# Where the gate's early load stands in the queue, fourth buffers for the output stage, and one more pair done with seven products

## The chip, the cores and the metric

The kernel runs on one core of one Trainium2 chip. Its engines work side by side and in order, each through its own list: TensorE (matrix products; PE in the profile, its weight loads PEld), VectorE (DVE), ScalarE (ACT), GpSimd (POOL) and SyncE (SP), which issues most of the DMA transfers. An engine that waits holds up what is behind it in its own list, and only that. The metric is the device time of one execution in microseconds; lower is better. All times below are microseconds unless marked ns. In the rows of the profile "L786" is line 786 of the kernel before.

## The reference

One decoder layer on 256 tokens of width 2048, everything in float32:

```python
h = rmsnorm(x, norm_g)                                   # (256, 2048)
shift, scale, gate = split(silu(c) @ ada_w + ada_b, 3)   # 3 x 2048
h = h * (1 + scale) + shift
b, cg, v, g = split(h @ w_in, 4)                         # w_in: 2048 x 4*4096
u = causal_depthwise_conv(cg * v, conv_w)                # width 3, per channel
y = b * u * silu(g)                                      # (256, 4096)
out = rmsnorm(x + gate * (y @ w_out), final_g)           # w_out: 4096 x 2048
```

The two large products dominate: h @ w_in with 128 MB of weights, and y @ w_out with 32 MB. `ada_w` is another 48 MB.

## The kernel before

**Precision.** Each large operand is split into a high part, which ScalarE casts to float32r (`split_hi`, L380), and a low part, the difference, which VectorE makes (`split_lo`, L385). A product is then three matmuls: high x high, high x low, low x high.

**The first product, first half.** The 4096 channels go in 32 columns of 128. The first 16 columns run in chunks while `ada_w` streams in (`part`, L573; bank `mm_s`); the orders of SyncE, VectorE and ScalarE there are written out by hand as strings of letters (L656 to L667). The tokens lie transposed in SBUF as `hT`, 16 blocks `k` of 128 model columns, each with a high and a low part (`tokens`, L322): blocks 0 to 13 in one tile with the tag "big", 14 and 15 in one with the tag "big2".

**The first product, second half** (L798 to L836, bank `mm_b`). Eight pairs of columns, for each the four quarters of `w_in` in the order c, v, g, b, for each quarter two loads of 1 MB with eight token blocks: 64 *pieces* of 48 matmuls with 256 columns. A piece is a load into `raw` (L804), its split into `hi` and `lo`, and the products; each piece goes twice through its eight blocks, once for each column of the pair. `raw`, `hi` and `lo` each go round three buffers (`w_tile`, L145). Behind each piece stand a call of `gate_piece` and one of `early_weights`.

`gate_piece` (L692) adds up the gate part of `ada_w`; at the end of each of four groups of 512 columns GpSimd folds the 128 partitions in seven steps, each with two DMAs and an addition (L713 to L717), and a last DMA adds the result to `gate_row` in DRAM (L719).

`early_weights` (L775) prepares parts of the output stage and stores them in DRAM (`made`). What is done behind which piece stands in `EARLY` (L761): behind pieces 35, 39, ... 55 the sums for pairs 10 to 15, behind piece 58 the load of the gate's last 512 columns on all partitions (`turned`, L786), behind 59 and 62 the weights of two units times that gate. The place of `turned` is also used by the fold. Outside the parts ordered by hand, a scheduler of the language, with its own picture of the times, chooses the order in each engine's list; `tc.add_manual_dep(..., after, ...)` orders two instructions of one engine without a semaphore.

**The second product** (the output stage, L838 on). `w_out` is used in pairs of 128-row blocks. `columns` (L943) runs 1024 output columns: the first 1024 with all 16 pairs, the second 1024 with 12 pairs, and the remaining weights of the second in four units of four blocks (`LAST`, each half of the columns for itself). A full pair is 24 matmuls with 512 columns. A pair in `SEVEN` or `SEVEN_2` is done as a Strassen-like scheme with seven block products, 21 matmuls (`seven`, L904): it needs sums of the tokens (`token_forms`, L729), sums of the weights (`sums_of`, L767) and splits of both the weights and the sums. In the first 1024 columns the sums of the weights are made on the spot; in the second they come from `made`. `gather` (L933) adds up the banks of the sevens.

Buffers of the output stage before: raw weights and sums share `wide_ring` (L857) in the first 1024 columns, three `lo` buffers and three places in `big`, the old token tile, up to n = 12, then the three `lo`; in the second `next_ring` (L1017), three `lo` and one place in `big`. Casts go round the three `hi`, low parts round the three `raw` buffers. `load_ends` (L863) puts loads for the end among the weights of the first 1024 columns: the gate's first half at n = 11 (`AT_END - 2`), half of `x` at n = 13, the final weights and the gate's second half at n = 14. The second half of `x` follows at n = 8 of the second columns (`AT_X`).

**The end.** With the gate already multiplied into the weights of the last 512 columns, the residual and the partial results go into PSUM first (`move`, L1042), and the last products are added there (`out_mm(po[t], ...)`), while VectorE and ScalarE do the rest of the final norm (`third`, `finish`).

Of the kernel before, what the change touches and what calls it, by code (L numbers as in the profile page):

```python
# [13 lines left out]
P = 128  # L14
D = 2048
# [102 lines left out]
def short_conv_layer(ctx: ExitStack, tc: tile.TileContext, x, c, norm_g, ada_w, ada_b, w_in, conv_w, w_out, final_g, out):  # L118
# [20 lines left out]

    nth = {"raw": 0, "hi": 0, "lo": 0}  # L140

    def pad(n, name, pool=wpool):
# [155 lines left out]
    rstd = const.tile([P, TT], F32, tag="rstd", name="rstd")  # L298
    junk = hpool.tile([P, TT, HX], F32, tag="big", name="junk")
    for t in range(TT):  # L300
# [16 lines left out]

    KB = KT - 2
    hT = hpool.tile([P, KB, 2 * T], F32R, tag="big", name="hT")
    hT2 = hpool.tile([P, KT - KB, 2 * T], F32R, tag="big2", name="hT2")  # L320

    def tokens(k, part):  # L322
        return (hT[:, k] if k < KB else hT2[:, k - KB])[:, part * T : (part + 1) * T]

# [351 lines left out]
    def gate_columns(c0, n):  # L676
        flat = gate_slots[c0 // 1024].rearrange("p h s f -> p (h s f)").bitcast(F32)
# [5 lines left out]
    def load_gate(j):  # L683

        c0 = j * 1024
        nc.sync.dma_start(gate_columns(c0, 1024), gate_row[0:1, c0 : c0 + 1024].partition_broadcast(P))

# [36 lines left out]
    SEVEN = range(8, 16)  # L724
    SEVEN_2 = range(10, 16)
    forms = {}
# [38 lines left out]
    passed = [0]  # L765

    def sums_of(b, s):  # L767
# [7 lines left out]
    def early_weights():  # L775

        while to_store:
            unit, sums = to_store.pop()
            made[unit] = dram.tile([P, SLOT], F32, tag=f"made{len(made)}", name="made")
            nc.scalar.dma_start(made[unit], sums)  # L780
        unit = EARLY.get(passed[0])
        passed[0] += 1
        if unit is None:
            return
        if unit == "gate":
            nc.sync.dma_start(turned, gate_row[0:1, 3 * W : 4 * W].partition_broadcast(P))  # L786
            return
        raw, sums = raw_tile("raw_u"), w_tile("lo", "sums_u")
        blocks, out = (v.rearrange("p (b f) -> p b f", f=W) for v in (raw, sums))
        if not isinstance(unit, int):  # L790
            load_o(raw, unit[1] * EP, EP, 3 * W, W)
            nc.vector.tensor_tensor(out=out, in0=blocks, in1=turned.unsqueeze(1).to_broadcast([P, EP, W]), op=ALU.mult)
        else:
            load_o(raw, 2 * unit, 2, 2 * W, 2 * W)
            list(sums_of(blocks, out))
        to_store.append((unit, sums))

    for ct in range(NS, NCT, 2):  # L798
        for q in QUARTERS:
            bank = psum.tile([P, CT, T], F32, tag="mm", name="mm_b")[:, 0:2]  # L800
            col = q * E + ct * P
            for kp in range(0, KT, KP):
                raw = raw_tile("raw")
                nc.sync.dma_start(  # L804
                    raw.rearrange("p (k f) -> p k f", k=KP),
# [32 lines left out]

    big = hpool.tile([P, 3 * D + W], F32, tag="big", name="big")
    xh = big[:, 0 : TT * D].rearrange("p (h t f) -> p h t f", h=2, t=TT)  # L840
    HD = D // 2

    def xr(t, c0, n):
        return xh[:, c0 // HD, t, c0 % HD : c0 % HD + n]

    def load_x(h):
        for t in range(TT):
            nc.sync.dma_start(xh[:, h, t], x[t * P : (t + 1) * P, h * HD : (h + 1) * HD])

    fg = big[:, TT * D : 3 * D]  # L850
    u2 = big[:, 3 * D :]
    ends = [z.rearrange("p a b f -> p (a b f)").rearrange("p (h f) -> p h f", h=2) for z in zs]

    places6 = [None] * 3 + [big[:, i * SLOT : (i + 1) * SLOT] for i in range(3)]
    taken, ending = [0], [False]

    def wide_ring(name):  # L857

        i = taken[0] % 6 if not ending[0] else 0
        taken[0] += 1  # L860
        return w_tile("lo", name) if places6[i] is None else places6[i]
# [12 lines left out]
    last_silu = ended_silu[0]  # L874
    warm2 = const.tile([P, 1], F32, tag="fs", name="warm2", bufs=2)
# [21 lines left out]
    def weighted(t, c0, n, pr, at):  # L897


        r = xr(t, c0, n)  # L900
        nc.scalar.activation(pr, r, AF.Square, scale=D**-0.5, accum_out=fsq[:, t, at : at + 1])
        nc.vector.tensor_tensor(out=r, in0=r, in1=fg[:, c0 : c0 + n], op=ALU.mult)

# [38 lines left out]

    def columns(c0, order, sevens, bank, p1, p6, p75, whole, loads=None, ring=None):  # L943


        for n, j in enumerate(order):
            raw = w_tile("raw", "raw_o") if n == 0 and c0 == 0 else ring("raw_o")
            ready = c0 > 0 and j in made
# [9 lines left out]
            if j in sevens:  # L958
                sums = ring("sums_o")
                if ready:  # L960
                    nc.sync.dma_start(sums, made[j])
                seven(j, raw, sums, ready, bank, p1, p6, p75, j == sevens[0], j == sevens[-1])
                if j == sevens[-1]:
                    gather(p1, p6, p75)
                continue
# [14 lines left out]
    def wide_bank(name):  # L980
# [5 lines left out]
        0, (0, 1, 8, 2, 9, 3, 10, 4, 11, 5, 12, 13, 6, 14, 15, 7), SEVEN,  # L986
        lambda t, d: wide[t][:, d], *extra_banks(), p75, True, load_ends, wide_ring,
    )
# [9 lines left out]
    def finish(t):  # L998
# [4 lines left out]
        for c0, n, vector in ((0, 512, True), (512, 512, False), (1536, 512, True), (1024, 512, False)):  # L1003
            dd = slice(c0, c0 + n)
            r = xr(t, c0, n)
            if c0 == 1536:
                nc.vector.scalar_tensor_tensor(out=r, in0=po[t], scalar=fs, in1=fg[:, dd], op0=ALU.mult, op1=ALU.mult)
# [7 lines left out]
    taken[0] = 0  # L1015

    def next_ring(name):  # L1017

        i = taken[0] % 4
        taken[0] += 1  # L1020
        return big[:, SLOT : 2 * SLOT] if i == 3 and taken[0] <= 12 else w_tile("lo", name)
# [88 lines left out]
```

## Time and profile before

| | us |
|---|---|
| runs without the profiler (3), median | 920.08 (919.80 to 920.12) |
| the profiled execution | 917.02 |
| its span, first to last instruction | 915.2 |
| TensorE busy | 888.6 (97%) |
| VectorE busy | 695.4 (76%) |
| ScalarE busy | 490.5 (54%) |
| GpSimd busy | 88.0 (10%) |

The profile of the chip lists every instruction with its start, its length and what ended the idle time before it. Busy shares are means over stages with different limits, so the stages are read one by one. By the first and last matmuls of each stage, the first half of the first product runs from 24.4 to 376.8, the second half from 376.9 to 740.2, and the output stage's matmuls from 740.23 to 907.9. In a row such as `L385 DVE TENSOR_TENSOR lo<-raw,hi 128x2048 ... x66 | 153.3, 2328 | 78.6 <-ACT hi L380 63.1` the numbers behind the first bar are the busy time of the group and the mean length of one in ns, and behind the second the idle time of the engine just before them and what ended most of it. A row `PE mm_b L545 <- ACT hi L380: 11.4, 1, 11.4` of the waits says who waited for whom, the sum, how often, and the longest.

### The profile page before, as it was taken

How to read it: one execution, taken by the hardware profiler on the slowest of the kernel's cores; microseconds unless marked ns; L12 is line 12 of the kernel's file. 1: busy time of each engine (PE TensorE's matmuls, PEld its weight loads, DVE VectorE, ACT ScalarE, POOL GpSimd, SP SyncE). 2: the span in 40 equal slices, each digit the busy share in tenths (PEclk: the TensorE clock that was granted, in tenths of full speed). 3: DMA queues.
4: the chain of work that ended last, by engine and by line, in shares of the span. 5: the costliest groups of instructions: out<-in, count | busy, mean ns of one | idle time of the engine just before them, and what ended most of it. 6: DMA issues, size and time to landing. Idle time of an engine off the chain costs nothing.

```text
span 915.2 us, 16520 instructions
## 1 busy us (share of the span) xinstructions
PE 888.6 (97%) x6977; PEld 849.9 (93%) x6977; DVE 695.4 (76%) x693; ACT 490.5 (54%) x436; POOL 88.0 (10%) x108
## 2 busy tenths in 40 slices
PE   7999999999999999999999999949999999999996
PEld 4999999999999999999999999949999988778885
DVE  5889998889987876858865786537667668999775
ACT  6768866565558765644344434234434454545553
POOL 0000000010000234410132012400000000000000
PEclk9999999999999999999999999979999999999999
DMA  9999999999997688777877889489889877686872
GB/s 307 368 370 365 365 321 354 341 363 351 380 344 258 189 279 238 237 215 222 271 230 219 273 270 307 142 286 301 290 286 289 306 264 244 197 294 235 302 280 92
DMA packets 164873, 257.29 MB, mean 281 GB/s; under 512 B 7668, under 2 KB 106580, under 8 KB 162624
## 3 DMA queue, kind: packets, MB, share of 16 engines
q1 hardware_dynamic: 159680, 239.89, 79.5%
q0 software_dynamic: 3840, 7.94, 3.2%
q10 hardware_dynamic: 1280, 8.43, 2.3%
q8 instruction: 54, 0.88, 0.4%
q14 instruction: 19, 0.16, 0.0%
HBM read 237.86 MB, written 10.50 MB: 271 GB/s over the span
## 4 chain that ended last, share of the span: by engine, by line
PE 79%; DMA 11%; DVE 4%; ACT 2%; POOL 2%; issue 1%; SPq 0%; ACTq 0%; POOLq 0%; DVEq 0%
PE mm_s L545 38%; PE mm_b L545 27%; PE mm_o L888 6%; PE mm L888 4%; DMA z<-gacc 3%; PE mm_w L888 3%; DMA at_g<-in_ada_w_dram 3%; DVE lo L385 2%; DMA at<-in_ada_w_dram 2%; ACT hi L380 2%; POOL gacc L717 1%; DMA raw_o<-in_sc_w_out_dram 1%; DMA raw<-in_sc_w_in_dram 1%; POOL z L715 0%; DVE gacc L711 0%
## 5 line engine op out<-in xcount | busy, mean ns | idle before, releaser
L545 PE MATMUL mm_b<-hT,hi 128*128 128x256 f32 x2048 | 349.9, 277 | 11.4 <-ACT hi L380 11.4
L545 PE MATMUL mm_s<-hT,hi 128*128 128x256 f32 x2048 | 336.3, 277 | 0.0
L545 PEld LDWEIGHTS mm_b<-hT,hi 128*128 128x128 f32 x2048 | 309.3, 188 | 11.6 <-ACT hi L380 11.6
L545 PEld LDWEIGHTS mm_s<-hT,hi 128*128 128x128 f32 x2048 | 299.7, 188 | 0.2
L545 PE MATMUL mm_b<-hT,lo 128*128 128x256 f32 x1024 | 283.4, 277 | 1.5 <-DVE lo L385 1.5
L545 PE MATMUL mm_s<-hT,lo 128*128 128x256 f32 x1024 | 261.7, 277 | 0.0
L380 ACT CAST hi<-raw 128x2048 fp32r<-128x2048 f32 (+1 forms) x66 | 123.8, 1876 | 206.9 <-PE mm_b L545 94.0
L385 DVE TENSOR_TENSOR lo<-raw,hi 128x2048 fp32r<-128x2048 f32 (+1 forms) x66 | 153.3, 2328 | 78.6 <-ACT hi L380 63.1
L545 PEld LDWEIGHTS mm_b<-hT,lo 128*128 128x128 f32 x1024 | 192.9, 188 | 1.8 <-DVE lo L385 1.8
L545 PEld LDWEIGHTS mm_s<-hT,lo 128*128 128x128 f32 x1024 | 182.7, 188 | 0.0
L385 DVE TENSOR_TENSOR lo<-raw_s,hi 128x2048 fp32r<-128x2048 f32 (+1 forms) x80 | 149.0, 1868 | 29.9 <-ACT hi L380 29.3
L380 ACT CAST hi<-raw_s 128x2048 fp32r<-128x2048 f32 (+2 forms) x81 | 124.0, 1541 | 70.2 <-PE mm_s L545 42.9
L515 DVE SCALAR_TENSOR_TENSOR gv<-at,silu_c,gv 128x512 f32<-128x512 f32 x105 | 78.8, 751 | 10.3 <-DMA at<-in_ada_w_dram 8.6
L568 ACT COPY acc<-mm_s 128x1024 f32<-128x1024 f32 x54 | 54.6, 1011 | 26.9 <-PE mm_s L545 26.8
L717 POOL TENSOR_TENSOR gacc<-gacc,z 128x512 f32<-128x512 f32 x28 | 44.2, 1577 | 103.4 <-DMA z<-gacc 103.4
L888 PE MATMUL mm_w<-hi,y 128*128 128x512 f32 x160 | 51.4, 390 | 0.3 <-ACT hi L380 0.3
L711 DVE SCALAR_TENSOR_TENSOR gacc<-at_g,silu_c,gacc 128x512 f32<-128x512 f32 x60 | 45.0, 749 | 7.4 <-DMA at_g<-in_ada_w_dram 6.3
L888 PE MATMUL mm_o<-hi,y 128*128 128x512 f32 x152 | 48.3, 389 | 0.0
L582 ACT COPY mm_s<-acc 128x1024 f32<-128x1024 f32 x38 | 38.6, 1015 | 2.6 <-DVE acc L571 1.8
L380 ACT CAST hi<-raw_o 128x2048 fp32r<-128x2048 f32 x14 | 26.7, 1909 | 22.1 <-DMA raw_o<-in_sc_w_out_dram 16.8
L385 DVE TENSOR_TENSOR lo<-raw_o,hi 128x2048 fp32r<-128x2048 f32 x14 | 32.1, 2289 | 6.8 <-ACT hi L380 6.7
L888 PEld LDWEIGHTS mm_w<-hi,y 128*128 128x128 f32 x160 | 30.0, 188 | 6.9 <-ACT hi L380 0.7
(191 smaller groups left out, 745.6 us busy)
## 6 DMA issues: line engine op xcount, KB each, us to landing
raw<-in_sc_w_in_dram SPq DMA_DIRECT2D x64, 1024.0 KB, 6.2
raw_s<-in_sc_w_in_dram SPq DMA_DIRECT2D x47, 1024.0 KB, 8.2
at<-in_ada_w_dram SPq DMA_DIRECT2D x126, 256.0 KB, 7.9
raw_o<-in_sc_w_out_dram SPq DMA_DIRECT2D x17, 1024.0 KB, 6.0
raw_s<-in_sc_w_in_dram SPq DMA_DIRECT2D x33, 512.0 KB, 7.2
at_g<-in_ada_w_dram SPq DMA_DIRECT2D x32, 512.0 KB, 8.2
raw_u<-in_sc_w_out_dram SPq DMA_DIRECT2D x8, 1024.0 KB, 5.7
made<-sums_u ACTq DMA_DIRECT2D x8, 1024.0 KB, 6.9
```

Of the source, the lines that this page charges most:

```text
L380: nc.scalar.copy(hi[:, :n], raw[:, :n])
L385: last_low[0] = nc.vector.tensor_tensor(out=lo[:, :n], in0=raw[:, :n], in1=hi[:, :n].bitcast(F32), op=ALU.subtract)
L515: nc.vector.scalar_tensor_tensor(out=gv, in0=at4[:, i], scalar=c_k, in1=gv, op0=ALU.mult, op1=ALU.add)
L545: mm = last_mm[0] = nc.tensor.matmul(dst, w, h[k], start=begins and left, stop=ends, skip_group_check=True)
L568: nc.scalar.copy(acc[ch, q], bank)
L582: nc.scalar.copy(bank, acc[ch, q])
L711: nc.vector.scalar_tensor_tensor(out=ga, in0=at3[:, i, :], scalar=s, in1=ga, op0=ALU.mult, op1=ALU.add)
L717: nc.gpsimd.tensor_tensor(out=ga, in0=ga, in1=turned, op=ALU.add)
L888: nc.tensor.matmul(dst, y[a], b, start=opens and i == 0, stop=ends and i == 2, skip_group_check=True)
```

## The change

- The gate's early load is put at piece 55 and tied: it can be issued only behind the load of that piece's weights. The units of `early_weights` come three pieces earlier (32, 36, ... 52; 56 and 60).
- The token tile `big` becomes four tiles b0 to b3. In the output stage b0, b1 and b2 serve as fourth buffers of `lo` (raw weights and sums), `hi` (casts) and `raw` (low parts). In the first 1024 columns all three kinds have four up to n = 10, then three; from n = 13 on `lo` has four again, with b1, up to n = 5 of the second columns. The rings of six and of four are gone.
- `x` goes into b0 and b1, the final weights and the gate's first half share b2 (`closing`), and the gate's second half goes into the first gate slot. The loads at n = 13 are half of `x`, half of the final weights and the gate's first half; at n = 8 of the second columns the other half of `x`, the gate's second half, and the other half of the final weights, which takes the place of the gate's first half.
- Pair 9 joins the sevens of the second columns; its sums are made on the spot. The order there becomes 0, 10, 1, 11, 2, 9, 3, 12, 13, 8, 14, 15; first and last of the sevens are taken from that order.

```diff
     def w_tile(kind, name, dtype=F32, i=None):
         if i is None:
-            i = nth[kind] % 3
-            nth[kind] += 1
+            size = 4 if kind in fourth else 3
+            i = nth[kind] % size
+            nth[kind] = i + 1
+        if i == 3:
+            return hpool.tile([P, SLOT + 64], dtype, tag=fourth[kind], name=name)[:, 16 : 16 + SLOT]
...
-    KB = KT - 2
-    hT = hpool.tile([P, KB, 2 * T], F32R, tag="big", name="hT")
-    hT2 = hpool.tile([P, KT - KB, 2 * T], F32R, tag="big2", name="hT2")
+    hT = [hpool.tile([P, SLOT + 64], F32R, tag=f"b{g}", name="hT") for g in range(3)]
+    hT += [hpool.tile([P, 4 * T], F32R, tag=tag, name="hT") for tag in ("b3", "big2")]
...
-    SEVEN_2 = range(10, 16)
+    SEVEN_2 = range(9, 16)
...
-    EARLY = {35 + 4 * i: j for i, j in enumerate(SEVEN_2)}
-    EARLY.update({58: "gate", 59: ("gated", LAST[0]), 62: ("gated", LAST[1])})
+    EARLY = {32 + 4 * i: j for i, j in enumerate(range(10, 16))}
+    EARLY.update({55: "gate", 56: ("gated", LAST[0]), 60: ("gated", LAST[1])})
...
         if unit == "gate":
-            nc.sync.dma_start(turned, gate_row[0:1, 3 * W : 4 * W].partition_broadcast(P))
+            load = nc.sync.dma_start(turned, gate_row[0:1, 3 * W : 4 * W].partition_broadcast(P))
+            tc.add_manual_dep(load.ins, last_load[0].ins.name, after, reason="the gate is done by then")
...
     def load_x(h):
+        xh.append(hpool.tile([P, TT, HD], F32, tag=f"b{h}", name="xr"))
...
+    def load_broadcast(c, src):
+        nc.sync.dma_start(closing[0][:, c : c + HD], src.partition_broadcast(P))
+
+    def load_fg(h):
+        load_broadcast(h * HD, final_g.rearrange("(o d) -> o d", o=1)[:, h * HD : (h + 1) * HD])
...
     def load_ends(n):
-        ending[0] = n >= AT_END
-        if n == AT_END - 2:
-            load_gate(0)
+        if n == AT_END - 3:
+            fourth.clear()
         elif n == AT_END:
             load_x(0)
-        elif n == AT_END + 1:
-            nc.sync.dma_start(fg, final_g.rearrange("(o d) -> o d", o=1).partition_broadcast(P))
-            load_gate(1)
+            closing.append(hpool.tile([P, D], F32, tag="b2", name="closing"))
+            load_fg(0)
+            load_broadcast(HD, gate_row[0:1, 0:HD])
+            fourth["lo"] = "b1"
+
+    fourth.update({"lo": "b0", "hi": "b1", "raw": "b2"})
...
+        in_turn = [j for j in order if j in sevens]
         for n, j in enumerate(order):
-            raw = w_tile("raw", "raw_o") if n == 0 and c0 == 0 else ring("raw_o")
+            raw = w_tile("raw" if n == 0 and c0 == 0 else "lo", "raw_o")
...
-                sums = ring("sums_o")
+                sums = w_tile("lo", "sums_o")
...
+    def load_last(n):
+        if n == AT_X - 3:
+            fourth.clear()
+        elif n == AT_X:
+            load_x(1)
+            nc.sync.dma_start(gate_columns(HD, HD), gate_row[0:1, HD:D].partition_broadcast(P))
+            load_fg(1)
...
-        2 * W, (0, 1, 10, 2, 11, 3, 12, 13, 8, 14, 15, 9), SEVEN_2,
-        lambda t, d: halves[d][:, t], *po, p75, False, lambda n: load_x(1) if n == AT_X else None, next_ring,
+        2 * W, (0, 10, 1, 11, 2, 9, 3, 12, 13, 8, 14, 15), SEVEN_2,
+        lambda t, d: halves[d][:, t], *po, p75, False, load_last,
```

More of the change, by code (lines that the diff above doesn't have):

```diff
@@ L140, in short_conv_layer @@
     nth = {"raw": 0, "hi": 0, "lo": 0}
+    fourth = {}
     def pad(n, name, pool=wpool):
@@ L298, in short_conv_layer @@
     rstd = const.tile([P, TT], F32, tag="rstd", name="rstd")
-    junk = hpool.tile([P, TT, HX], F32, tag="big", name="junk")
+    junk = hpool.tile([P, TT, HX], F32, tag="b0", name="junk")
     for t in range(TT):
@@ L765, in short_conv_layer @@
     passed = [0]
+    last_load = [None]
     def sums_of(b, s):
@@ L836, in short_conv_layer @@
         gate_piece()
[L839 to L840 removed]
     HD = D // 2
+    xh = []
     def xr(t, c0, n):
[L844 removed]
+        return xh[c0 // HD][:, t, c0 % HD : c0 % HD + n]
     def load_x(h):
+        xh.append(hpool.tile([P, TT, HD], F32, tag=f"b{h}", name="xr"))
         for t in range(TT):
[L848 to L861 removed]
+            nc.sync.dma_start(xh[h][:, t], x[t * P : (t + 1) * P, h * HD : (h + 1) * HD])
+    u2 = hpool.tile([P, W], F32, tag="b3", name="u2")
+    closing = []
+    def load_broadcast(c, src):
+        nc.sync.dma_start(closing[0][:, c : c + HD], src.partition_broadcast(P))
+    def load_fg(h):
+        load_broadcast(h * HD, final_g.rearrange("(o d) -> o d", o=1)[:, h * HD : (h + 1) * HD])
+    ends = [z.rearrange("p a b f -> p (a b f)").rearrange("p (h f) -> p h f", h=2) for z in zs]
     def load_ends(n):
[L865 to L867 removed]
+        if n == AT_END - 3:
+            fourth.clear()
         elif n == AT_END:
             load_x(0)
[L870 to L872 removed]
+            closing.append(hpool.tile([P, D], F32, tag="b2", name="closing"))
[3 more added lines that the diff above has]
+    fourth.update({"lo": "b0", "hi": "b1", "raw": "b2"})
     last_silu = ended_silu[0]
@@ L941, in gather, with columns @@
         add(ends[1][:, 0], p75[:, 1], ends[1][:, 1])
-    def columns(c0, order, sevens, bank, p1, p6, p75, whole, loads=None, ring=None):
+    def columns(c0, order, sevens, bank, p1, p6, p75, whole, loads=None):
+        in_turn = [j for j in order if j in sevens]
         for n, j in enumerate(order):
-            raw = w_tile("raw", "raw_o") if n == 0 and c0 == 0 else ring("raw_o")
+            raw = w_tile("raw" if n == 0 and c0 == 0 else "lo", "raw_o")
             ready = c0 > 0 and j in made
@@ L958, in columns @@
             if j in sevens:
-                sums = ring("sums_o")
+                sums = w_tile("lo", "sums_o")
                 if ready:
                     nc.sync.dma_start(sums, made[j])
-                seven(j, raw, sums, ready, bank, p1, p6, p75, j == sevens[0], j == sevens[-1])
-                if j == sevens[-1]:
+                seven(j, raw, sums, ready, bank, p1, p6, p75, j == in_turn[0], j == in_turn[-1])
+                if j == in_turn[-1]:
                     gather(p1, p6, p75)
```

24 lines of the change are left out of this document (10 added, 14 removed).

## The prediction

> **What bounds the kernel now.** I read four views in this order: the page's slices, TensorE's waits, SyncE's waits, and windows over the stages.
>
> ```profile
> PE   7999999999999999999999999949999999999996
> PEclk9999999999999999999999999979999999999999
> ```
>
> TensorE is busy to nine tenths or more in every slice but the first, the last and slice 27 (22.9 us each), where the granted clock dips too. So two things are worth anything: matmuls taken away, and that slice. TensorE's waits of over 1 us behind the start are two, and SyncE's waits between 500 and 620 us name their cause:
>
> ```profile
> PE mm_b L545 <- ACT hi L380: 11.4, 1, 11.4
> PE mm_b L545 <- DVE lo L385: 1.5, 1, 1.5
> SPq L786 <- DMA z<-gacc: 15.9, 1, 15.9
> SPq L786 <- DMA gate_row<-gacc: 3.8, 1, 3.8
> ```
>
> The timelines of SyncE and TensorE there (start, length, instruction), and the span of the stage's matmuls:
>
> ```profile
> 575.93 0.37 SPq L755 DMA_DIRECT2D raw_u<-in_sc_w_out_dram  x1
> 596.25 0.34 SPq L786 DMA_DIRECT2D z<-gate_row  x1
> 596.70 12.07 SPq L804 DMA_DIRECT2D raw<-in_sc_w_in_dram  x4
> ...
> 606.10 0.80 PE L545 MATMUL mm_b<-hT,hi 128*128 128x256 f32 x2 [11.43 <-ACT hi L380]
> ...
> L545 PE MATMUL mm_b<-hT,hi x2048: 276/276/579, 376.9 to 740.0; 128*128 128x256 f32 x187
> ```
>
> SyncE issues in order. From 576.30 (575.93 + 0.37) it stood before the gate's early load (L786) until GpSimd's last fold of the gate had been written at 596.25. Behind it stood the weights of the next pieces (L804). They left at 596.70, and TensorE, out of weights, stood still. The written place of L786 is behind piece 58 of 64, but at 48 matmuls of 0.1133 us (below) a piece lasts 5.44 us, and TensorE had done (594.67 - 376.9) / 5.44 = 40 pieces when it stopped (606.10 - 11.43 = 594.67): the scheduler had put L786 some 18 pieces ahead.
>
> ```profile
> 238.67 138.39 PE mm_s L545 x1221
> 897.05 10.89 PE mm L888 x48
> 594.00:612.00 18.00, 5.04 (x27) 4.54 (x27) 5.59 (x5) 3.80 (x2) 0.73 (x1) 0.62 0.82 265
> 612.00:740.20 128.20, 128.20 (x1133) 128.20 (x1132) 82.97 (x73) 54.02 (x43) 0.00 (x0) 1.00 0.89 292
> 740.20:797.00 56.80, 56.74 (x251) 46.50 (x250) 49.41 (x41) 29.05 (x19) 0.00 (x0) 1.00 0.70 233
> 797.00:820.00 23.00, 21.72 (x93) 16.76 (x92) 21.49 (x15) 12.78 (x9) 0.00 (x0) 1.00 0.79 275
> 820.00:908.00 88.00, 87.93 (x388) 72.26 (x386) 70.75 (x58) 46.40 (x39) 0.00 (x0) 1.00 0.68 239
> ```
>
> The first two rows are of the chain: 138.39 / 1221 = 0.1133 us per 256-column matmul, 10.89 / 48 = 0.2269 per 512-column one. The rest are windows: length, then busy time (and count) of TensorE, its weight loads, VectorE, ScalarE, GpSimd, then clock, DMA share and GB/s. In 594 to 612 there is room for 18.00 / 0.1133 = 158.9 matmuls and 27 ran: 132 x 0.1133 = **14.95 us lost**, of which 11.4 + 1.5 are the waits and 2.0 the lower clock (0.62) after them. Behind it TensorE has no gap up to 740.2, with DMA at 0.89. In the output stage only 797 to 820 shows loss: 23.00 / 0.2269 = 101.4 fit, 93 ran, so 1.9 us, and VectorE is at 21.49 of 23.00 there.
>
> On the clock the row says 2.0 us. The Trainium skill (TensorE: Matmul & The Clock Gate, Part 1) has the clock at half for some 3.4 us after an idle window, which would make it 1.7 and the loss 14.6.
>
> **The change, part by part.** *The tie.* L786 may now be issued only behind the load of piece 55. TensorE reaches that piece at 376.9 + 55 x 5.44 = 676 without the stall, and the load leaves two to three pieces earlier, from 660. The gate's row is written at 596, so L786 finds it ready and nothing behind it (the raw of the first gated unit, piece 56) waits. Cover gone, it would cost what it costs now. **-14.95**, with up to 3 more if the timed runs' extra 3.06 us lies in this stall.
>
> *Units three pieces earlier.* The same loads, sums and stores, at 32, 36, ... 52, 56, 60. The stretch after 612 carried a unit every four pieces with no TensorE gap, so 0; at most one 1.5 us wait of the kind above, where the first unit now meets the last gate loads.
>
> *The seventh ready pair.* Pair 9 becomes 21 matmuls in place of 24: 3 x 0.2269 = **-0.68**. Its sums aren't stored ahead, so VectorE makes them:
>
> ```profile
> L385 DVE TENSOR_TENSOR lo<-raw_o,hi 128x2048 fp32r<-128x2048 f32 x14 | 32.1, 2289 | 6.8 <-ACT hi L380 6.7
> L918 DVE TENSOR_TENSOR lo<-raw_o,hi 128x1536 fp32r<-128x1536 f32 x11 | 19.3, 1753 | 5.9 <-ACT hi L917 5.9
> L769 DVE TENSOR_TENSOR sums_o<-raw_o 128x1024 f32<-128x1024 f32 x5 | 6.1, 1219 | 0.0
> L772 DVE TENSOR_TENSOR sums_o<-raw_o,sums_o 128x512 f32<-128x512 f32 x5 | 3.5, 690 | 0.1
> L380 ACT CAST hi<-raw_o 128x2048 fp32r<-128x2048 f32 x14 | 26.7, 1909 | 22.1 <-DMA raw_o<-in_sc_w_out_dram 16.8
> ```
>
> 1.22 + 0.69 + 0.69 (L773 as L772) + 1.75 + 2.29 = 6.64 us where 2.29 stood, so +4.35 on VectorE against 4.76 of TensorE for the pair. VectorE has the room: 70.75 of 88.00 us from 820 to 908. At nothing here, up to 4.35 if that cover is gone.
>
> *The turn into the output stage.* The rotation now goes on into the fourth buffers. I counted uses of raw: 1 at the start, 64 in the chunks (47 loads of 1 MB, and 33 half ones, two to a place), 64 pieces, 8 units: 137, so number 136 mod 3 = 1 was the last. The stage's first raw takes number 2, and the first pair's low part number 3: b2, the old tokens 8 to 11.
>
> ```profile
> raw_s<-in_sc_w_in_dram SPq DMA_DIRECT2D x47, 1024.0 KB, 8.2
> raw_s<-in_sc_w_in_dram SPq DMA_DIRECT2D x33, 512.0 KB, 7.2
> ...
> 732.54 2.29 DVE L385 TENSOR_TENSOR lo<-raw_o,hi 128x2048 fp32r<-128x2048 f32 x1 [0.63 <-ACT hi L380]
> 739.75 0.88 SPq L755 DMA_DIRECT2D big<-in_sc_w_out_dram  x2
> 740.23 0.39 PE L888 MATMUL mm_w<-hi,y 128*128 128x512 f32 x1
> ```
>
> Before, that low part was ready at 734.83, 5.4 us ahead of the stage's first matmul (740.23), while the loads into the token tile left only at 739.75. The last piece goes through its eight token blocks twice, so b2 comes free 12 matmuls before its end, 1.36 us; the low part takes 2.29 and is 0.9 late, the second matmul having needed it 0.23 in. Between 0 (other products first) and 1.5 I take **+0.6**. VectorE's work behind it (L830 and the last pair's y) slips as much, and pair 15 comes 15th, some 14 x 5.1 = 71 us later.
>
> *First 1024 columns.* Raw and sums go round four buffers where there were six; casts and low parts four where there were three, up to n = 10. Both gate loads leave this stage's queue:
>
> ```profile
> SPq L686 <- PE mm L888: 9.6, 2, 5.3
> DMA to landing us min/median/max: 4.1/5.3/7.4
> ```
>
> The second row is that of the token tile as a buffer, 735 to 830. Two pairs, one full and one of seven, use three raw places, cost VectorE 2.29 + 6.64 = 8.93 and TensorE 45 x 0.2269 = 10.2. A fourth hi and lo let VectorE run ahead by 1.3 a round, up to one split, which should halve the 1.9 lost at the neighbours 12, 13 and 14, 15. Against it, with four raw places and three from n = 10 the load of pair 6 leaves only when pair 12's sums are split, and VectorE can be without work for some 2 us. Between -1.9 and +3 I take **-1.0**.
>
> *The end.* The order puts pair 9 sixth, so its matmuls no longer stand between pair 15 and the two last units:
>
> ```profile
> 878.54 2.29 DVE L385 TENSOR_TENSOR lo<-raw_o,hi 128x2048 fp32r<-128x2048 f32 x1 [0.23 <-ACT hi L380]
> 894.93 2.28 DVE L385 TENSOR_TENSOR lo<-raw_o,hi 128x2048 fp32r<-128x2048 f32 x1
> 846.00:880.00 34.00, 22.07 (x11) 1.00 0.88 308
> ```
>
> The second gated piece's low part was done at 897.21 and needed at 897.05 + 12 x 0.2269 = 899.77, 2.6 us in hand. 24 x 0.2269 = 5.45 of cover goes, and 2.29 of VectorE work with it (the row at 878.54): 2.6 - 5.45 + 2.29 = -0.6. VectorE then ends the third quarter later as well; I give it 0.4. Between 0 and +4 I take **+1.0**. Behind pair 8's load also stand two more 512 KB loads (gate, half of the final weights) with DMA at 0.88 (last row: window, VectorE, clock, DMA): 1.05 MB at 308 GB/s is 3.4 us, hence the 4. The Trainium skill (DMA: Bandwidth & Descriptors, Measured) gives a 1 MB load 341 GB/s, by which it would be 3.1.
>
> Sum: -14.95 - 0.68 + 0.6 - 1.0 + 1.0 = **-15.0 us**. The profiled execution took 917.02 (span 915.2, 1.8 around it), so 902.0. The median shown is 920.08, 3.06 above; nothing in the trace places that, and I leave it there: **905.0**.
>
> **The rivals.** *The buffers do all they may*: no turn cost, no loss in the first columns, a covered end, and part of the 3.06 in the stall. -14.95 - 0.68 - 1.9 - 2 = -19.5, 900.5. For it: the loss sits where VectorE is full. Against it: the raw ring shrinks.
>
> *The output stage starves*: +1 at the turn, +3 in the first columns, +4 at the end: -7.6, 912. For it: the casts' idle time before L380 is put down to DMA for 16.8 us, and VectorE gives up its slack at the end. Against it: a full pair in the first columns may land up to 10.2 - 1.9 = 8.3 us after issue without a loss, and the longest took 7.4.
>
> *A second queue block, slower than before.* Half of the final weights goes (n = 8 of the second columns) into the place where the gate's first half is read by the residual (L894), an instruction of late priority. SyncE must stand until VectorE has done both, with the weights of 14, 15 and the last units behind.
>
> ```profile
> 831.54 1.22 DVE L894 TENSOR_TENSOR z<-z,gate 128x1024 f32<-128x1024 f32 x1
> 862.50 0.80 SPq L848 DMA_DIRECT2D big<-in_x_dram  x2
> ```
>
> Before, the read was over 30 us ahead of that point (862.50 - 832.76). The old block shows the price: 19.95 us of standing (576.30 to 596.25) lost 14.95, so 5.0 were covered. Slower than before starts where the standing passes 15 + 2 + 5 = 22 us, that is where L894 comes 52 us later than now; 60 us later gives 920 + 13 = 933. A wait of this length also pays the low clock. Unlikely: VectorE stood idle for 12 of the 34 us after 846.
>
> *The tie doesn't do it*: the gate's row isn't ready at 660, or something else holds the queue as long. Then about 919. The fold would have to end 64 us late.
>
> **How the numbers follow.** Forecast (902.5 to 908) 0.50; buffers do all (898 to 902.5) 0.18; starving (908 to 917) 0.25; tie without effect 0.03; second block 0.04. To leave out no more than 0.2, the range runs from 899.5 to 911.0: all of the small case but its end, the forecast, and the nearer half of the starving one. A measurement of this kernel can tell about 0.2%, 1.8 us, from no change: faster 0.93, same 0.03, slower 0.04.
>
> **What would show it.** Right: no TensorE wait near 595, clock full in all slices from the second, L786 behind the load of piece 55 and waiting for nothing, the first L888 some 15 us earlier (near 725), 723 of them in place of 726. The turn: a TensorE wait on DVE lo of under 1 us at the first L888. First columns: less than 1.9 lost around pairs 12 to 15. The end: the wait on the second gated low part, some 0.6. Wrong: a SyncE wait of over 8 us anywhere behind 560, ScalarE's casts waiting for raw_o in the first columns for longer than before, or a TensorE wait over 2 us.

## The result and the profile after

| | before | after |
|---|---|---|
| first measurement, same chip, six runs each, median | 919.62 (915.45 to 920.12) | **905.05** (904.12 to 908.66) |
| ratio | | 0.9858 [0.9833, 0.9884] |
| a second chip, median | 916.99 | 908.81 (907.24 to 910.23) |
| ratio there | | 0.9912 [0.9897, 0.9926] |
| the profiled execution (span) | 917.02 (915.2) | 907.24 (905.5) |

The change is faster on both chips, by 14.6 us on one and 8.2 on the other. The two intervals don't meet: the size of the gain differs between the two batches, each on a chip of its own; its sign does not. The profiled spans differ by 9.7 us, and that is what the traces have to explain.

The page's slices of after, the rows of TensorE and of the granted clock:

```profile
PE   7999999999999999999999999999999999999996
PEclk9999999999999999999999999999999999999999
```

The hole in slice 27 is gone, and the dip of the clock with it. SyncE's timeline there (start, length, instruction), and GpSimd's at the end of the fold (from here on, line numbers in rows are those of the kernel that the row is from):

```profile
649.52 9.15 SPq L808 DMA_DIRECT2D raw<-in_sc_w_in_dram  x3
659.03 0.34 SPq L789 DMA_DIRECT2D z<-gate_row  x1
```
```profile
601.99 0.82 POOL L721 DMA_DIRECT2D gate_row<-gacc  x1 [0.30 <-POOL gacc L719]
```

The gate's load (now L789) leaves at 659.03, directly behind weights and 57 us after the last DMA of the fold was issued. It waits for nothing. The windows of after by stage (length, then busy time and count of TensorE, weight loads, VectorE, ScalarE, GpSimd, then clock, DMA share, GB/s):

```profile
594.00:612.00 18.00, 17.21 (x152) 17.02 (x151) 12.42 (x13) 9.26 (x7) 2.11 (x2) 1.00 0.94 303
612.00:728.00 116.00, 115.67 (x1015) 115.11 (x1014) 72.89 (x65) 50.36 (x39) 0.00 (x0) 1.00 0.85 282
728.00:785.00 57.00, 57.00 (x253) 47.17 (x252) 51.48 (x42) 28.97 (x18) 0.00 (x0) 1.00 0.71 238
785.00:808.00 23.00, 22.85 (x100) 18.36 (x99) 21.69 (x15) 12.72 (x9) 0.00 (x0) 1.00 0.77 272
808.00:897.00 89.00, 84.37 (x365) 67.52 (x364) 70.13 (x58) 44.12 (x36) 0.00 (x0) 1.00 0.65 221
```

Where 27 matmuls ran between 594 and 612, 152 run now, at full clock. The row of 785 to 808 is fuller than before's was (100 matmuls in 23 us for 93). But the last row has a loss that was not there: 84.37 busy of 89.00 us, where before had 87.93 of 88.00 at the corresponding place. TensorE's waits over the whole execution say for what:

```profile
PE mm L891 <- DVE lo L390: 1.5, 2, 0.8
PE mm_o L891 <- DVE lo L390: 1.5, 2, 0.8
PE mm L891 <- ACT hi L920: 1.4, 2, 1.0
PE mm_b L550 <- DVE lo L390: 0.8, 1, 0.8
...
PE mm_w L891 <- DVE lo L390: 0.3, 1, 0.3
```

The first three lie in the second 1024 columns, the fourth in the first product, the last at the turn; none is over 1.0 us. The stages, from the tiles' groups of after (duration min/median/max, first to last start), and of before for the last two:

```profile
L550 PE MATMUL mm_b<-hT,hi x2048: 276/276/283, 376.9 to 725.9; 128*128 128x256 f32 x187
L891 PE MATMUL mm_w<-hi,y x160: 387/389/397, 726.1 to 808.8; 128*128 128x512 f32 x160
L891 PE MATMUL mm<-hi,y x62: 388/389/500, 726.6 to 897.9; 128*128 128x512 f32 x62
```
```profile
L888 PE MATMUL mm_w<-hi,y x160: 387/389/497, 740.2 to 824.5; 128*128 128x512 f32 x160
L888 PE MATMUL mm<-hi,y x60: 388/389/402, 746.1 to 907.5; 128*128 128x512 f32 x60
```

Cut at the first and the last start of `mm_w` (before: 740.2 and 824.5) and the last of `mm`, this gives the account of the study:

| | first product, second half | first 1024 columns | second 1024 columns |
|---|---|---|---|
| before | 376.9 to 740.2: 363.3 | 84.3 | 83.0 |
| after | 376.9 to 726.1: 349.2 | 82.7 | 89.1 |
| difference | **-14.1** | **-1.6** | **+6.1** |

Together -9.6, the difference of the spans but for 0.1.

### The profile page after: what moved, and what is told of

The parts are those of the page before. It is cut to its first block, busy times and chain, and to the rows that moved or that the text cites. A ratio compares the mean times of both kernels' runs of the same rounds, so it can differ in the third digit from the quotient of the medians.

```text
span 905.5 us, 16518 instructions
## 1 busy us (share of the span) xinstructions
PE 887.0 (98%) x6974; PEld 847.4 (94%) x6974; DVE 702.3 (78%) x697; ACT 492.6 (54%) x437; POOL 93.1 (10%) x108
## 4 chain that ended last, share of the span: by engine, by line
PE 83%; DMA 7%; DVE 6%; ACT 2%; issue 1%; SPq 0%; ACTq 0%; DVEq 0%
PE mm_s L550 39%; PE mm_b L550 35%; PE mm_w L891 5%; DVE lo L390 3%; PE mm L891 3%; DMA at<-in_ada_w_dram 2%; DMA raw<-in_sc_w_in_dram 2%; ACT hi L385 2%; PE mm_o L891 2%; DMA sums_o<-made 2%; DMA raw_o<-in_sc_w_out_dram 1%; DVE lo L921 1%; DVE sums_o L772 0%; DVE z L897 0%; DVE sums_o L775 0%
## 5 line engine op out<-in xcount | busy, mean ns | idle before, releaser
L719 POOL TENSOR_TENSOR gacc<-gacc,z 128x512 f32<-128x512 f32 x28 | 47.9, 1712 | 109.2 <-DMA z<-gacc 109.2
L390 DVE TENSOR_TENSOR lo<-raw_o,hi 128x2048 fp32r<-128x2048 f32 x17 | 38.7, 2288 | 15.5 <-ACT hi L385 9.0
L385 ACT CAST hi<-raw_o 128x2048 fp32r<-128x2048 f32 x17 | 32.4, 1908 | 29.8 <-DMA raw_o<-in_sc_w_out_dram 10.5
L891 PE MATMUL mm_o<-hi,y 128*128 128x512 f32 x140 | 45.1, 390 | 0.2 <-DVE z L939 0.2
L390 DVE TENSOR_TENSOR lo<-sums_o,hi 128x2048 fp32r<-128x2048 f32 x15 | 34.4, 2290 | 14.1 <-ACT hi L385 14.1
L385 ACT CAST hi<-sums_o 128x2048 fp32r<-128x2048 f32 x15 | 28.6, 1905 | 29.0 <-DVE sums_o L776 12.4
```

Source lines behind the costliest of these rows:

```text
L385: nc.scalar.copy(hi[:, :n], raw[:, :n])
L390: last_low[0] = nc.vector.tensor_tensor(out=lo[:, :n], in0=raw[:, :n], in1=hi[:, :n].bitcast(F32), op=ALU.subtract)
L719: nc.gpsimd.tensor_tensor(out=ga, in0=ga, in1=turned, op=ALU.add)
L891: nc.tensor.matmul(dst, y[a], b, start=opens and i == 0, stop=ends and i == 2, skip_group_check=True)
```

## The experiments

Two theories stood at the start. One: the tie is the whole gain, and the second 1024 columns lose because they have too few places for raw weights and sums (three from n = 5 on, where before went on with four through all the sevens). The rival: what is lost there is pair 9, whose sums VectorE now makes. The kernels of a batch ran on one chip with runs of before; each of the three batches had its own.

For the reading, two measures of each kernel's profile: the length of the first 1024 columns, and the matmuls missing in three stretches counted from the last `mm_w`, against the 90, 178 and 90 that before and the first profile of the tie alone run there (one matmul is 0.2269 us). Times are medians, beside the tie alone of the same batch. Each count comes from one execution: between the three of the tie alone it moves by up to 3, between the two of after by 5 in the middle and by 17 at the end.

| kernel | pair 9 | order | buffers | time | over the tie alone | first columns | missing in 0-20, 20-60, 60-80 us |
|---|---|---|---|---|---|---|---|
| tie alone (three batches) | full | old | old | 901.88, 903.81, 902.00 | 0 | 83.8, 83.9, 83.8 | 0, 0, 0; 0, 3, 0; 0, 2, 0 |
| after, first profile | on the spot | new | new | 905.05 | | 82.7 | 7, 13, 10 |
| after again | on the spot | new | new | 908.81 | +5.0 | 82.7 | 7, 8, 27 |
| rest without the tie | on the spot | new | new | 919.44 | | 82.7 | 7, 13, 6 |
| six ready pairs | full | old | new | 906.33 | +4.5 | 82.7 | 8, 9, 0 |
| order alone | full | new | new | 905.11 | +1.3 | 82.7 | 7, 0, 12 |
| pair 9 on old buffers | on the spot | new | old | 906.56 | +4.7 | 83.8 | 3, 2, 14 |
| fourth place longer | on the spot | new | new, longer | 904.67 | +2.7 | 82.7 | 7, 1, 6 |
| the same, six pairs | full | old | new, longer | 907.25 | +5.2 | 82.9 | 9, 8, 5 |

### The tie alone, three times

Before with nothing but the tie and the earlier units:

```diff
-    EARLY = {35 + 4 * i: j for i, j in enumerate(SEVEN_2)}
-    EARLY.update({58: "gate", 59: ("gated", LAST[0]), 62: ("gated", LAST[1])})
+    EARLY = {32 + 4 * i: j for i, j in enumerate(range(10, 16))}
+    EARLY.update({55: "gate", 56: ("gated", LAST[0]), 60: ("gated", LAST[1])})
...
-            nc.sync.dma_start(turned, gate_row[0:1, 3 * W : 4 * W].partition_broadcast(P))
+            load = nc.sync.dma_start(turned, gate_row[0:1, 3 * W : 4 * W].partition_broadcast(P))
+            tc.add_manual_dep(load.ins, last_load[0].ins.name, after, reason="the gate is done by then")
```

> The kernel before with the tie and the earlier units alone; output stage as before. Theory A (the whole gain is the stall, the output stage gives back what it gains): 14.0 to 15.5 us faster than the kernel before, no TensorE wait over 1.5 us between 500 and 740, the clock full there, and the output stage from its first to its last matmul within 1 us of the 167.8 us of before. Rival B (the 3 us by which the timed runs of before exceed its profiled one lie in the stall): 17 to 18 us faster.

> The tie and the earlier units alone, beside the changed kernel on the same chip: 2 to 4 us below it if the rest of the change costs time, within 1 us of it if not. The second columns lose under 0.5 us.

> The tie and the earlier units alone on this chip, as the measure for the other three: 0.984 to 0.987 of the kernel before.

The ratios are 0.9840 [0.9808, 0.9872], 0.9861 [0.9846, 0.9876] and 0.9829 [0.9806, 0.9853], against 916.83, 916.99 and 917.61 of before: 15.0, 13.2 and 15.6 us. All of what the change brings comes from the tie with the earlier units, and more; the tie with the units at their old places wasn't run. Gains of 17 to 18 us, as the rival had them, are excluded. Windows of the first of the three:

```profile
785.00:808.00 23.00, 22.15 (x96) 17.43 (x95) 21.73 (x17) 11.93 (x8) 0.00 (x0) 1.00 0.81 288
808.00:893.00 85.00, 85.00 (x376) 70.30 (x375) 68.72 (x56) 44.94 (x37) 0.00 (x0) 1.00 0.66 234
```

From 808 to the last matmul TensorE never stops, where after stood 4.6 us; from 785 to 808 it runs 96 matmuls for after's 100. So the old buffers are worse in the first columns and better in the second.

### The rest without the tie

```diff
-            tc.add_manual_dep(load.ins, last_load[0].ins.name, after, reason="the gate is done by then")
```

> The changed kernel without the tie; the gate's load is again free to move ahead, and stands in SyncE's list behind the third of the early units. Theory A: SyncE stands for about 21 us from 583 on, TensorE stands for 11 to 14 us near 605 and then runs at a lower clock for some us; 13 to 16 us slower than the changed kernel, that is within 3 us of the kernel before. Rival (the earlier place in the program is what counts, not the tie): within 2 us of the changed kernel.

Measured 919.44, ratio 1.0022 [1.0003, 1.0040]. SyncE's timeline and then its waits:

```profile
582.81 0.37 SPq L757 DMA_DIRECT2D raw_u<-in_sc_w_out_dram  x1
598.57 0.34 SPq L789 DMA_DIRECT2D z<-gate_row  x1
```
```profile
SPq L789 <- DMA z<-gacc: 11.4, 1, 11.4
...
SPq L789 <- DMA gate_row<-gacc: 3.7, 1, 3.7
```

The block is back: 15.4 us of standing (583.18 to 598.57) in place of 19.95, although the load is written behind piece 55. The scheduler puts it early without the edge. TensorE's window there:

```profile
594.00:618.00 24.00, 14.59 (x105) 14.10 (x105) 9.40 (x11) 7.22 (x6) 2.10 (x2) 0.79 0.72 234
```

24.00 / 0.1133 = 211.8 matmuls fit and 105 ran, 12.1 us lost. The first columns are 82.7 long and the second columns miss 7, 13 and 6: both effects on the output stage are there without the tie.

### Six ready pairs, and the order alone

After with pair 9 a full pair, in the old order and in the new (the second kernel has only the first edit):

```diff
-    SEVEN_2 = range(9, 16)
+    SEVEN_2 = range(10, 16)
...
-        2 * W, (0, 10, 1, 11, 2, 9, 3, 12, 13, 8, 14, 15), SEVEN_2,
+        2 * W, (0, 1, 10, 2, 11, 3, 12, 13, 8, 14, 15, 9), SEVEN_2,
```

> The changed kernel with six pairs of seven in the second columns, in the order of before; the buffers as changed. Theory C (the second columns starve because four raw places become three from n = 5 on): the matmuls behind the first 1024 columns still lose 4 to 6 us, and the time is that of the changed kernel plus 0.7, within 1.5 us. Theory D (pair 9's sums and the order make the loss): the loss goes to under 2 us, and the time is 3 to 5 us below the changed kernel.

> The changed kernel with its order in the second columns, but pair 9 full, without sums. If the order makes the loss (its last full pair no longer covers the end, and the sevens come sooner), the second columns still lose 4 to 6 us; if pair 9's sums on VectorE make it, they lose about 2 us, as with six pairs in the old order, and the time is 1.5 to 3.5 us below the changed kernel.

906.33 and 905.11. With six pairs and the old order 17 matmuls (3.9 us) are still missing, more than theory D allowed: the seventh pair is not the whole loss on the new buffers. The order alone is 3.7 below after in the same batch: the seven products of pair 9 save 0.68 us of matmuls and cost 3.7 net. (Its profiled execution, 906.07, was one of its longer ones, so its 19 missing matmuls are more than the 1.3 of its median.) By the table, each order has its own place of loss on the new buffers. The new order misses nothing in the middle and 12 matmuls in the last stretch. The chain of waits of the order alone there (start, length, what), and SyncE's timeline of it and of the tie alone:

```profile
863.67 7.21 DMA raw_o<-in_sc_w_out_dram
...
872.91 2.30 DVE lo L390
...
875.26 10.93 PE mm_o L891 x47
```
```profile
863.67 3.48 SPq L757 DMA_DIRECT2D raw_o<-in_sc_w_out_dram  x2
```
```profile
855.65 8.45 SPq L755 DMA_DIRECT2D raw_o<-in_sc_w_out_dram  x3
```

The load at 863.67 is the first of the last units, the next after pair 15's. In the old order pair 9's 24 matmuls (5.45 us) stand before the units, and three loads leave from 855.65; here nothing stands between pair 15 and a weight that lands at 870.88.

### Pair 9 on the old buffers

The tie alone, with pair 9 among the sevens and the new order, on before's buffers: four places all through.

```diff
-    SEVEN_2 = range(10, 16)
+    SEVEN_2 = range(9, 16)
...
-        2 * W, (0, 1, 10, 2, 11, 3, 12, 13, 8, 14, 15, 9), SEVEN_2,
+        2 * W, (0, 10, 1, 11, 2, 9, 3, 12, 13, 8, 14, 15), SEVEN_2,
```

Its pair 9 multiplies with token sums whose place the gate's second half has already overwritten, so that part of the output isn't the reference's.

> The tie, the seventh pair and its order, with the buffers of before (six places, then four). Theory C: the second columns lose under 2 us, the first columns lose some 2 us around pairs 12 to 15 as before, time 1 to 3 us below the changed kernel. Theory D: the second columns lose 4 to 6 us as in the changed kernel, and the time is 1 to 2 us above it.

Measured 906.56. In all 19 matmuls (4.3 us) are missing, as many as theory D had, but not where the sums are made. Only 2 matmuls are missing between 20 and 60 us, where pair 9's sums are made, but 14 in the last stretch: with four places pair 9 itself is hidden, the missing cover at the end is not.

### The fourth place two pairs longer

After with the loads at n = 8 of the second columns moved to n = 10, so that the fourth place stays to n = 7; then the same edit on the six pairs in the old order.

```diff
-    AT_X = 8
+    AT_X = 10
```

> The changed kernel with the fourth raw place kept two pairs longer in the second columns (to n = 7, the loads for the end at n = 10 in place of 8). If the number of places for raw weights and sums is what starves the second columns once pair 9's sums hold one of them, they lose 2 to 4 us less than in the changed kernel, and the time is 2 to 4 us below it. If VectorE's work for pair 9 itself is late, or the order alone, the time stays within 1 us.

> Six pairs and the old order in the second columns, the changed buffers, and the fourth place kept to n = 7 with the loads for the end at n = 10. If places are the cause, the 1.8 us that the second columns lost with six pairs go to under 1, and the time is within 1 us of the tie alone; if not, it is 2 to 4 us above the tie alone.

904.67 for the first, 2.7 above the tie alone, where after was 5.0 above it on another chip. The chain of waits of after there:

```profile
833.43 1.68 DVE lo L921
...
835.51 4.95 DMA raw_o<-in_sc_w_out_dram
...
842.12 1.77 DVE lo L921
...
843.91 7.33 DMA sums_o<-made
...
851.35 1.92 ACT hi L385
...
853.28 2.30 DVE lo L390
...
855.60 6.80 DMA sums_o<-made
...
866.76 5.29 DMA raw_o<-in_sc_w_out_dram
...
876.43 10.93 PE mm_o L891 x47
```

Pair 9's low part (L921, behind its sums) frees its place, and only then does a load leave. From there each load leaves when another place has been split, and lies on the path itself: load, cast and low part, 843.91 to 855.60, 11.7 us a round. With three places that is 3.9 us per tile of weights. Pairs 3, 12, 13, 8, 14, 15 use ten tiles (two for a pair of seven) and give TensorE 132 x 0.2269 = 30.0 us, 3.0 per tile; four places would give 2.9. With the place kept longer the same chain reads

```profile
831.03 5.00 PE mm_o L891 x22
...
842.02 6.90 DMA sums_o<-made
...
872.05 10.95 PE mm_o L891 x47
```

It leaves TensorE's own work later, at 836.03, with one load less on it, and the last stretch begins 4.4 us earlier (0.7 of that because the stage does). Of the 13 matmuls missing in the middle 12 are back, of the 10 at the end 4. The edit also moves the load of `x` from 822.93 to 837.05; the chain of after doesn't pass through that load. On the six pairs the edit did nothing (907.25; 9, 8 and 5 missing): a miss for the places in that order. The chain of the six pairs runs in such rounds too (loads at 830.78, 842.16 and 854.78), without any sums of pair 9. With the fourth place kept it leaves TensorE's work only at 847.11, and 8 matmuls are still missing; what is short in that order stays open.

### A seventh unit, and another order in the first columns

Pair 9's sums stored ahead like the others', on after; and on the tie alone, the full pairs of the first 1024 columns spread otherwise:

```diff
-    EARLY = {32 + 4 * i: j for i, j in enumerate(range(10, 16))}
+    EARLY = {28 + 4 * i: j for i, j in enumerate(range(9, 16))}
```
```diff
-        0, (0, 1, 8, 2, 9, 3, 10, 4, 11, 5, 12, 13, 6, 14, 15, 7), SEVEN,
+        0, (0, 1, 8, 2, 9, 10, 3, 11, 4, 12, 5, 13, 6, 14, 15, 7), SEVEN,
```

> The changed kernel with pair 9's sums made ahead as well, behind piece 28 (the units at 28, 32, ... 52), and loaded from DRAM like the others. If VectorE's 2.6 us for the sums are what is late, the second columns lose 1 to 3 us less than in the changed kernel. If the loads are late (1.75 MB for a ready pair in place of 1 MB for one on the spot), they lose as much or up to 3 us more.

> The tie alone, with the pairs of the first 1024 columns in an order that puts the two neighbouring sevens 9, 10 and 14, 15 far apart (0 1 8 2 9 10 3 11 4 12 5 13 6 14 15 7). If the 2.3 us lost in the first columns come from VectorE at two neighbouring pairs of sevens with one full pair between, 1 to 2 us of them go, and the time is 1 to 2 us below the tie alone. If the early neighbours meet VectorE's work for the last y, the time is up to 2 us above it.

The seventh unit took 918.53, ratio 1.0019 [1.0008, 1.0030]: the gain is gone, at a place that the experiment wasn't about. Its windows at the turn:

```profile
730.00:734.00 4.00, 1.28 (x8) 0.76 (x7) 3.09 (x6) 2.09 (x2) 0.00 (x0) 0.93 0.87 275
734.00:738.00 4.00, 1.65 (x3) 0.83 (x3) 3.11 (x5) 3.54 (x2) 0.00 (x0) 0.50 1.02 417
738.00:742.00 4.00, 3.11 (x7) 2.01 (x8) 3.81 (x3) 0.68 (x2) 0.00 (x0) 0.50 0.24 97
```

Some 11 matmuls run in 8 us, and the clock falls to half. In the chain there a load of `w_out` leaves only at 725.36, when a matmul of the first product has released its place, and lands at 730.82. One more unit shifts the rotation of three buffers by one; that this is the cause was not tried by itself. Its second columns miss 7, 6 and 8, but behind such a stop that says little of pair 9.

The other order took 902.68 (900.18 to 906.78) beside 902.00 (900.50 to 903.53) for the tie alone on the same chip. The times don't tell the two apart. In its profile the first columns take 83.2 us for 83.8, 0.6 less where 1 to 2 were expected; and TensorE waits twice, 4.1 us in all, for low parts in the first product, which the edit doesn't touch.

### After once more, beside the tie alone

> The changed kernel once more, beside the tie alone on the same chip. If the rest of the change costs time, it is 2 to 4 us above the tie alone; if the gap between the two came from the chips, they agree within 1 us. In the profile the second columns, from the first mm_o matmul to the last matmul, lose 4 to 6 us against 0.2269 us per matmul.

908.81 (907.24 to 910.23), and 903.81 (901.71 to 904.77) for the tie alone: 5.0 us, with no overlap of the runs and more than the 2 to 4 expected. **The tie with the earlier units is faster than before and than the whole change**, and in each batch it had the lowest median. In this profile 42 matmuls (9.5 us) are missing, where 4 to 6 us were expected; the last stretch alone misses 27, for 10 in the first profile. Windows there:

```profile
870.00:876.00 6.00, 4.18 (x16) 2.37 (x14) 2.81 (x2) 2.71 (x3) 0.00 (x0) 1.00 0.85 282
876.00:878.00 2.00, 0.18 (x2) 0.17 (x2) 2.00 (x2) 1.81 (x1) 0.00 (x0) 1.00 0.42 164
878.00:880.00 2.00, 2.00 (x6) 1.58 (x7) 1.97 (x4) 0.09 (x1) 0.00 (x0) 0.55 0.55 123
880.00:882.00 2.00, 2.00 (x7) 1.58 (x6) 2.00 (x2) 1.52 (x1) 0.00 (x0) 0.60 0.98 401
```

A wait of 1.8 us for a low part, and behind it 4 us with the clock at 0.55 to 0.60.

## Why the prediction held, and where it did not

The time was 905.05, the forecast 905.0. By its steps one term was wrong by some 3 us, a loss of 1.6 was not in it at all and one term was chosen too small; what had been left unplaced stood in for them. That the two times agree so closely is luck.

- **The tie, -14.95: right.** Alone it gave 13.2 to 15.6 on three chips. In the profile the first product got 14.1 shorter, with one wait of 0.8 for the earlier units (predicted: at most one of 1.5; one execution of the other order in the first columns had two, 4.1 together). The load left at 659.03 (from 660), the first matmul of the output stage at 726.1 (near 725).
- **The 3.06 us between the profiled execution and the median shown: not in the stall.** The prediction left them unplaced, in the time. Before's medians in the later batches were 916.8, 917.0 and 917.6, next to its profiled 917.02, so the difference was one between batches and executions. The rival that put part of it into the stall was wrong. The working's own figure, 902.0 for the profiled execution, stands against 907.24: 5.2 too low.
- **The turn, +0.6: right in mechanism, half the size.** The timeline of after:

```profile
724.96 4.49 DVE L390 TENSOR_TENSOR lo<-raw_o,hi 128x2048 fp32r<-128x2048 f32 x2 [6.51 <-PE mm_b L550]
...
727.31 0.49 PE L891 MATMUL mm_w<-lo,y 128*128 128x512 f32 x1 [0.33 <-DVE lo L390]
```

  VectorE waited for the old token blocks, began the low part 1.1 us before the first product's end, and TensorE waited 0.33.
- **The first 1024 columns, -1.0: right.** With the turn's 0.33 in it this stage went from 84.3 to 82.7, -1.6 where -0.4 was predicted for both. The tie alone has 83.8 to 83.9 and every undisturbed kernel with the new buffers 82.7 to 82.9, so 1.1 of it belongs to the buffers.
- **The seventh pair, -0.68: the step that failed.** Its 4.35 us of VectorE work were costed "at nothing here, up to 4.35 if that cover is gone", from VectorE's 70.75 busy of 88.00 us. The matmuls are gone; but 13 matmuls (2.9 us) are missing between 20 and 60 us, 8 in the second profile. In this order it takes two things: without pair 9's sums none are missing there, with the fourth place kept longer one, on the old buffers two. VectorE's mean share was the wrong cover. A load waits for a low part to free its place, pair 9's sums delay that low part, and three places have no round to spare. The prediction counted places and landing times in the first columns and not in the second.
- **The start of the second columns, not in the prediction.** 7 matmuls (1.6 us) are missing in the first 20 us of every kernel with the new buffers and new order, 8 or 9 in the old order, 3 or none with the old buffers. So the buffers give back here what they gain in the first columns. VectorE's and TensorE's timelines of after there:

```profile
814.40 2.36 DVE L897 TENSOR_TENSOR z<-z,closing 128x1024 f32<-128x1024 f32 x2
816.68 2.36 DVE L898 TENSOR_TENSOR xr<-xr,z 128x1024 f32<-128x1024 f32 x2
818.95 2.29 DVE L390 TENSOR_TENSOR lo<-raw_o,hi 128x2048 fp32r<-128x2048 f32 x1
...
821.29 0.50 PE L891 MATMUL mm_o<-lo,y 128*128 128x512 f32 x1 [0.67 <-DVE lo L390]
```

  VectorE does the four operations of the first columns' residual in one go, and the low part that TensorE needs stands behind them. In the tie alone low parts stand between the same operations (at 815.56 and 819.50), and TensorE doesn't wait. This stop and one for `gather` (0.22) cost some 1.2 of the 1.6 us: matmuls start at 820.21 and 821.29, and at 809.47 and 810.08, where 0.2269 apart was due. In the old order TensorE waits 1.56 us for a cast instead. Whether VectorE's order comes from the place that the final weights now share with the gate's first half (their load, written at n = 8, left at 816.79, right behind the read L897), or from one of the rings, wasn't tried.
- **The end, +1.0 (0 to +4): the lost cover was right, what comes late was not, and the size was too small.** With pair 9 sixth, its matmuls no longer cover the units. Late was not the second gated low part, but the first unit's plain weights. Nor did the loads for the end stand where the working had them: n = 8 of the new order is pair 13, not pair 8, and they left at 816.79 and 822.93, ahead of pair 3's weights. 10 matmuls (2.3 us) are missing in after's last stretch, 6 to 14 in the other kernels with this order, and 27 (6.1 us) where the low clock came on top; in the old order none, but for 5 in one kernel.
- **The rivals.** "The output stage starves" had the kind right, a load landing late, but put +3 into the first columns, which gained. "A second queue block" came to 1.9 us of SyncE's waits, where 22 would have been needed:

```profile
SPq L858 <- DVE z L897: 1.9, 1, 1.9
```

  The working has that kernel at 933 for a read 60 us later; by its own figures 30 us of standing, less 5.0 covered and 15.0 gained, are +10, some 930. "The tie doesn't do it" is excluded by the tie alone. Of the signs of being wrong, a SyncE wait of over 8 us is there in after (19.2), but it is the store of the output at the end, as long before (19.0), and says nothing here; TensorE's longest wait behind the start was 1.0.

Against the tie alone the account closes in the profiles. For the first of each, 7 + 13 + 10 matmuls missing are 6.8 us, less 1.1 in the first columns and 0.68 of matmuls gives 5.0; the output stage, from the first `mm_w` to the last `mm`, took 171.8 and 166.8. For the second, 42 missing against 3 are 8.85 us, less 1.2 and 0.68 gives 7.0; the stages took 174.7 and 167.6. The forecast met the time because the unplaced 3.06 and the scatter between batches covered this loss. Sign and range rested on the one large term that rows carried.

## What to carry to other kernels

Look first for an in-order queue with one waiting load on it: 20 us of standing in SyncE's list cost 15 us, and one ordering edge, run here with the units three pieces earlier, removed it without taking any work away. Run such an edge apart from the rest: here the rest cost 5 us on the chip where both ran. Where loads wait for places, set the round of a place (landing, cast, low part: 11.7 us here) over the number of places against TensorE's time per tile, and don't conclude from an engine's mean idle share that a few us more on it are hidden.

## What the runs showed of the hardware

- One kernel differed from batch to batch, each on one chip, by as much as the effects under study: after 905.05 and 908.81, before 916.8 to 919.6. Whether the chip makes this wasn't separated. Differences of 2 to 3 us could only be read within one batch.
- A wait of 1.8 us was followed by a low clock in one kernel and not in another. In the second profile of after 1.8 us, with 1.8 more of idle time in the 6 us before, were followed by 4 us at 0.55 to 0.60. With pair 9 on the old buffers a wait of 1.83 us (at 876.47), with 0.7 more in the 6 us before, left it at 1.00, and so did 1.56 us with six pairs and 0.2 to 1.0 us in after. The Trainium skill (TensorE: Matmul & The Clock Gate, Part 1) has the slow clock last some 3.4 us after an idle window of about that length; the 4 us agree roughly, and the idle time agrees only if both pieces are counted. Counted so, the kernel that kept its clock had 2.5 us, less than such a window, which fits; no run was made to try it.
- The gate's load, 256 KB to all partitions, took 9.7 us to land in after and 4.3 in before, by the profile's table of DMA issues.
